# A planner's durations, a shared port and the readiness of q and k, in a transformer trunk whose attention heads are woven into its projections

## The chip, the cores and the metric

The kernel runs on one core of one Trainium2 chip. The metric is the device time of one execution in microseconds (us). Engines are called PE (TensorE), DVE (VectorE), ACT (ScalarE), POOL (GpSimd) and SP (SyncE, which only issues DMAs here).

## The reference

Two layers of a trunk on 512 tokens with 1024 features, in float32:

```python
for l in range(DEPTH):                                   # 2
    x = x + 0.5 * swiglu_ffn(x, ...)                     # 1024 -> 2816 -> 1024
    h = rms_norm(x, mix_norm[l])
    aq, ak, av, bq, bk, bv, cq, ck, cv, cg, gates = jnp.split(h @ w_in[l], split_points, axis=-1)
    y_a = diff_attention(qa, ka, va, lam, lam_init, a_subln[l])   # 4 heads, two softmaxes each, QK norm, rotary
    y_b = chunk_attention(qb, kb, vb, b_rel_bias[l])              # 8 heads, bias by distance, QK norm
    y_c = retention(qc, kc, vc, cg, c_out_norm[l])                # 4 heads, decay, output gate
    merged = (g[:, :, 0] * (y_a @ w_branch_a[l]) + g[:, :, 1] * (y_b @ w_branch_b[l])
              + g[:, :, 2] * (y_c @ w_branch_c[l]))               # g: sigmoid of the gate projections
    x = x + merged @ w_out[l]
    x = x + 0.5 * swiglu_ffn(x, ...)
```

y_a and y_c are normalised over the 128 features of each head before they are multiplied by their branch's weights.

## The kernel before

**Tiles.** Activations lie transposed, 128 features by 512 tokens to a tile. Each float32 operand is split into a high and a low part in fp32r, and each product becomes three matmuls: high by high, high by low, low by high (`mm3`, L230; in the profile bank<-xh,wh, xl,wh and xh,wl). The weights stream through SBUF once, in 422 chunks of 128x1024: SP loads a chunk (wr), ACT writes its high part (wh), DVE its low part (wl). Three chunks can be loaded ahead and three split (RAW, SPL). All 128x512 tiles come out of one ring of 72 (`big`, L170): a new tile is written only when everything that reads the tile 72 before it has ended, copies by DMA too. PE's results go to eight PSUM banks.

**Stages.** A layer is an FFN, a mixer and an FFN. The mixer (`mixer`, L914) makes the projections of q, k and v for A, then for B (`tokens`), then for the three branches. `branch` (L1029) first makes eight gate projections of 24 matmuls each; for branch 0 four projections of C's gates follow (`c_gates`: cg, cs); then come the branch's own matmuls over the four finished outputs ys, as bank<-yh,wh, yl,wh and yh,wl, three by four for each of eight output tiles. Between branch 0 and branch 1 the q, k and v of C are projected. At the end stands the projection by w_out.

**Side programs.** All that belongs to the heads is written as generators, which yield wherever they would wait:

- `prep` (L606) normalises and rotates the projected q or k (z), transposes it on PE (bank<-ident,z), splits it (qh, ql) and copies the halves by DMA into stacked tiles qk (`stack`, `twice`, copies at L661); `c_prep` (L997) does the same for C, with its copies at L1012.
- `a_head`, `b_head` and `c_head` (L775, L814, L849) multiply q by k, make the softmax or the decay (e, m, s), transpose it (bank<-ident,e to pt), multiply it by the values (vh, vl, or vv for B) and, for A and C, sum the squares of the output with a matmul against ones (`settle_head`).
- `finish` (L751) waits for a pair of heads, takes the inverse root of their sums of squares (ss; v, n, r, nine steps of 128x512 on DVE, `rsqrt_wide`), spreads it by DMA (rh<-r, L763), multiplies the heads' outputs by it (yu) and, for C, by the gate, and splits them (yh, yl). When the last pair is done it sets the flag yA or yC. B's heads set yB by themselves.

**What sets the order.** Every engine runs its instructions in the order in which they are written, and `Model` (L52) decides that order while the kernel is being built. It keeps a clock for each engine, adds a duration for each instruction (`note`, L89), and knows when each tile is ready (`ready`) and when a bank is free. After each projection matmul, `tick` (L249) lets a side program take a step if the model holds its operands for ready, if DVE and ACT are less than BACKLOG = 5000 ns behind PE, and if PE's pacing allows it. A step says what it waits for by what it yields: `then(...)`, `product(...)` with 1600 ns more, or `room(...)`, which asks for a free bank too and adds 800 ns. All of these are waits of the model; what an engine really waits for are the semaphores of its operands. A tile sent by DMA counts as ready 2500 ns after the latest of the clocks (`sent`, L85).

If the flag of a branch has not been set when its matmuls are due, `branch` calls `drain` (L301), which lets the side programs run with no projection matmul between them until the flag is there:

```python
if flag not in self.flags:
    self.drain(flag)
```

Of the kernel before, what the change touches and what calls it, by code (L numbers as in the profile page):

```python
# [35 lines left out]
class Queue:  # L36


    def __init__(self, model, name, engine):
        self.model, self.name, self.engine = model, name, engine  # L40
# [11 lines left out]
class Model:  # L52
# [3 lines left out]
    def __init__(self):  # L56
        self.t = dict(pe=0.0, dve=0.0, act=0.0, pool=0.0)
        self.wrote = {}
        self.read = {}
        self.slots = [0.0] * 8  # L60
        self.owner = {}

    @staticmethod
# [18 lines left out]
        end, by = max(self.read.get(self.key(ap), [(0.0, "pe")]))  # L82
        self.slots[self.owner.pop(self.key(ap))] = end + self.LAG[by]

    def sent(self, ap, wait=2500):  # L85

        self.wrote[self.key(ap)] = max(self.t.values()) + wait, "pe"

    def note(self, eng, op, named):  # L89
        aps = {k: a for k, a in named.items() if isinstance(a, bass.AP)}  # L90
        outs = [aps[k] for k in ("out", "accum_out") if k in aps]
        ins = [a for k, a in aps.items() if k not in ("out", "accum_out")]
        n = max(math.prod(a.shape[1:]) for a in outs[:1] + ins) if eng != "pe" else math.prod(outs[0].shape[1:])
        by_row = any(k in aps for k in ("scalar", "scalar1", "scale", "bias"))
        if "dma" in op:
            for a in outs:
                self.wrote[self.key(a)] = max(self.t[eng], self.t["pe"]) + 2500, eng
            return
        if eng == "pe":
            if op == "transpose":  # L100
                d = 109
            elif named["rhs"].dtype == F32R:
                d = n / 2.37 if n >= 256 else 213
            else:
                d = max(n, 64) * 1.7
        elif eng == "dve":
            plain = not any(a.space == bass.MemoryType.PSUM for a in ins + outs)
            d = 68 + n / (1.92 if op == "tensor_scalar" and plain else 0.96)
            d += 60 * by_row
        elif eng == "act":  # L110
            d = (50 if aps["in_"].space == bass.MemoryType.PSUM else 93) + n * 0.834 + 93 * by_row
        else:
            d = 100 + n * 2.2
        at = max([self.t[eng]] + [self.ready(a, eng) for a in ins])
        self.t[eng] = at + d
        for a in outs:
            self.wrote[self.key(a)] = at + d, eng
        for a in ins:
            if a.space == bass.MemoryType.PSUM:
                self.read.setdefault(self.key(a), []).append((at + d, eng))  # L120


def then(*aps):

    return aps, False, 0
# [7 lines left out]
def room(*aps):  # L133

    return aps, True, Kernel.MARGIN


class Kernel:
# [636 lines left out]
    def a_head(self, h, st):  # L775
        nc = self.nc
        es = self.weights()
        sums = {}

        def combine(i, e):  # L780
            s0, s1 = sums[i]
            for s in sums[i]:
                nc.vector.reciprocal(s, s)
            nc.vector.tensor_tensor(out=s1, in0=s1, in1=st["nlam"], op=ALU.mult)
            nc.vector.tensor_scalar(out=es[i], in0=es[i], scalar1=s0, scalar2=None, op0=ALU.mult)
            nc.vector.scalar_tensor_tensor(out=es[i], in0=e, scalar=s1, in1=es[i], op0=ALU.mult, op1=ALU.add)

        yield room(*(st[s][2 * h + c][0] for s in "qk" for c in range(2)))
        for i in range(NB + 1):
            if i < NB:  # L790
                bank = self.scores(st["q"][2 * h], st["k"][2 * h], i)
                yield then(bank)
                n = P * (i + 1)
                s = sums[i] = [self.small(1, "s") for _ in range(2)]
                self.softmax(bank, i, self.mask, s[0], es[i])
                yield room()
                bank = self.scores(st["q"][2 * h + 1], st["k"][2 * h + 1], i)
            if i:
                yield then(e)
                combine(i - 1, e)  # L800
            if i < NB:
                yield then(bank)
                e = self.big(F32, "e1")[:, 0:n]
                self.softmax(bank, i, self.mask, s[1], e)
                if i < NB - 1:
                    yield room()
        yield room(*es)
        pt = yield from self.transposed(es)
        yield "av"
        o = yield from self.values(pt, st["v"], slice(h * P, (h + 1) * P))  # L810
        yield from self.settle_head(o, st, h)
        self.flags.add(f"A{h}")

    def b_head(self, h, st):  # L814
        nc = self.nc
        tb = self.table()
        es = self.weights()
        yield room(*(st[s][h][0] for s in "qk"))
        for i in range(NB):
            bank = self.scores(st["q"][h], st["k"][h], i)  # L820
            yield then(bank)
            s = self.small(1, "s")
            e = es[i]
            self.softmax(bank, i, tb, s, e)
            yield then(e)
            nc.vector.reciprocal(s, s)
            nc.vector.tensor_scalar(out=e, in0=e, scalar1=s, scalar2=None, op0=ALU.mult)
            if i < NB - 1:
                yield room()
        self.fetch_table()  # L830
        yield room(*es)
        pt = yield from self.transposed(es)
        yield "bv"
        o = yield from self.values_b(pt, st["v"], h)
        if st["yu"][h // 2] is None:
            st["yu"][h // 2] = self.big(F32, "yb"), self.big(F32, "yb")
        y, t = st["yu"][h // 2]
        own, other = (slice(64 * i, 64 * i + 64) for i in (h % 2, 1 - h % 2))
        nc.scalar.activation(out=t[own], in_=o[other], func=AF.Copy)
        yield then(t)  # L840
        nc.vector.tensor_tensor(out=y[own], in0=o[own], in1=t[own], op=ALU.add)
        self.free(o)
        st["n"][h // 2] += 1
        if st["n"][h // 2] == 2:
            st["y"][h // 2] = yield from self.split_side(y)
            if None not in st["y"]:
                self.flags.add("yB")

    def c_head(self, h, st):  # L849
        nc = self.nc  # L850
        q, k = st["q"][h], st["k"][h]
        dt = self.table()
        pt = self.turned()
        yield room(q[0], k[0], k[1])
        for j in range(NB):
            bank = self.bank()
            n = S - j * P
            w = max(n, 256)
            o = slice(j * P, (j + 1) * P)
            self.dots(bank[:, 0:w], (k[0][:, o], k[1][:, o]), (q[0][:, S - w:S], q[1][:, S - w:S]))  # L860
            yield then(bank)
            if j < NB - 1:
                d = self.big(F32, "d")
                nc.vector.tensor_tensor(out=d[:, 0:n], in0=bank[:, 0:n], in1=dt[:, 0:n], op=ALU.mult)
                self.free(bank)
                hi, lo = pt[j]
                yield then(d)
                nc.scalar.activation(out=hi, in_=d[:, 0:n], func=AF.Copy)
                yield then(hi)
                nc.vector.tensor_tensor(out=lo, in0=d[:, 0:n], in1=hi.bitcast(F32), op=ALU.subtract)  # L870
            else:
                nc.vector.tensor_tensor(out=pt[j], in0=bank[:, w - n:w], in1=dt[:, 0:n], op=ALU.mult)
                self.free(bank)
            yield room()
        self.fetch_table()
        yield "cv"
        o = yield from self.values(pt, st["v"], slice(h * P, (h + 1) * P))
        yield from self.settle_head(o, st, h)
        self.flags.add(f"C{h}")
# [333 lines left out]
```

## Time and profile before

| | us |
|---|---|
| median of 3 runs | 2547.5 (2544.88 to 2548.47) |
| the profiled execution | 2552.16 |
| its span, from the first to the last instruction | 2550.4 |
| PE busy | 2517.2 |
| DVE busy | 1375.7 |
| ACT busy | 919.8 |
| POOL busy | 138.3 |

The mean clock granted to TensorE over the span is 0.996 of full speed. In rows of the timeline the columns are start, duration, engine, line, operation, out<-in, and in brackets the idle time ahead and what ended it. Most instructions have L48, the line of the helper through which all engines are called; they are told apart by their tiles. Rows of groups give the count, busy time and mean in ns of one, then the idle time before them.

### The profile page before, as it was taken

Reading aid. Unit: us, or ns where it says so; the run is one execution under the profiler, and the core shown is the slowest. Engines: PE = TensorE matmul, PEld = TensorE weight load, DVE = VectorE, ACT = ScalarE, POOL = GpSimd, SP = SyncE. Lnnn points to the kernel's source line nnn. Section 1 sums busy time; section 2 is a strip of 40 time slices with the busy share of each in tenths; the row PEclk is TensorE's granted clock in tenths of the full one; section 3 lists DMA queues with packets and bytes.
Section 4 is the critical chain, followed back from the end, with each engine's and each line's share of the span. In section 5 each row is a group of like instructions: output and inputs, shape, how many; then the busy total and the mean of one; then the engine's idle time right before and its main releaser. Section 6 shows DMA issues by size and latency. Waiting matters only on the chain.

```text
span 2550.4 us, 28931 instructions
## 1 busy us (share of the span) xinstructions
PE 2517.2 (99%) x11226; PEld 2054.4 (81%) x11226; DVE 1375.7 (54%) x2180; ACT 919.8 (36%) x1397; POOL 138.3 (5%) x104
## 2 busy tenths in 40 slices
PE   9999999999999999999999999999999999999999
PEld 7888887887878888888888888878878788888887
DVE  6334338776758653433353433477767576543332
ACT  4333224553443433332233332245534433333321
POOL 0000101000102100000000001010001021000000
PEclk9999999999999999999999999999999999999999
DMA  5333344527433433333333333344274324333332
GB/s 167 92 99 91 118 130 123 134 83 190 115 105 83 140 99 99 92 99 94 96 92 98 91 97 114 120 133 123 85 196 113 106 76 146 99 94 99 91 111 71
DMA packets 96617, 280.91 MB, mean 110 GB/s; under 512 B 13536, under 2 KB 14944, under 8 KB 96480
## 3 DMA queue, kind: packets, MB, share of 16 engines
q1 hardware_dynamic: 95760, 278.45, 38.2%
q8 instruction: 88, 1.44, 0.2%
q10 hardware_dynamic: 720, 0.62, 0.1%
q14 instruction: 49, 0.40, 0.0%
HBM read 237.08 MB, written 6.29 MB: 95 GB/s over the span
## 4 chain that ended last, share of the span: by engine, by line
PE 93%; DVE 3%; SPq 2%; DMA 1%; issue 0%; ACT 0%; DVEq 0%
PE bank L48 93%; SPq L661 1%; SPq L1012 1%; DVE wl L48 1%; DMA qk<-ql 1%; DVE e L48 0%; DMA x<-in_xt 0%; DVE n L48 0%; DVE g L48 0%; DVE z L48 0%; DVE pt L48 0%; DVE r L48 0%; DMA qk<-yh 0%; DVE ql L48 0%; ACT wh L48 0%
## 5 line engine op out<-in xcount | busy, mean ns | idle before, releaser
L48 DVE TENSOR_TENSOR wl<-wr,wh 128x1024 fp32r<-128x1024 f32 x422 | 530.8, 1259 | 705.7 <-ACT wh L48 703.6
L48 PE MATMUL bank<-xh,wh 128*128 128x512 f32 x1920 | 758.8, 395 | 0.0
L48 PE MATMUL bank<-xl,wh 128*128 128x512 f32 x1920 | 757.6, 395 | 0.1
L48 PE MATMUL bank<-xh,wl 128*128 128x512 f32 x1920 | 756.3, 394 | 0.0
L48 ACT ACTIVATE wh<-wr 128x1024 fp32r<-128x1024 f32 x422 | 445.4, 1056 | 775.2 <-PE bank L48 671.2
L48 PEld LDWEIGHTS bank<-xh,wh 128*128 128x128 f32 x1920 | 361.9, 188 | 78.2 <-ACT xh L48 1.2
L48 PEld LDWEIGHTS bank<-xl,wh 128*128 128x128 f32 x1920 | 362.0, 189 | 77.9 <-DVE xl L48 1.7
L48 PEld LDWEIGHTS bank<-xh,wl 128*128 128x128 f32 x1920 | 361.9, 188 | 77.7
L48 PE MATMUL bank<-ph,wh 128*128 128x512 f32 x704 | 276.6, 393 | 0.0
L48 PE MATMUL bank<-pl,wh 128*128 128x512 f32 x704 | 276.6, 393 | 0.0
L48 PE MATMUL bank<-ph,wl 128*128 128x512 f32 x704 | 276.6, 393 | 0.0
L48 PE MATMUL bank<-wl,xh 128*128 128x512 f32 x448 | 179.2, 400 | 0.0
L48 PE MATMUL bank<-wh,xh 128*128 128x512 f32 x448 | 178.8, 399 | 0.0
L48 PE MATMUL bank<-wh,xl 128*128 128x512 f32 x448 | 178.2, 398 | 0.0
L48 PEld LDWEIGHTS bank<-ph,wh 128*128 128x128 f32 x704 | 132.4, 188 | 29.6
L48 PEld LDWEIGHTS bank<-ph,wl 128*128 128x128 f32 x704 | 132.4, 188 | 29.4
L48 PEld LDWEIGHTS bank<-pl,wh 128*128 128x128 f32 x704 | 132.4, 188 | 29.4
L48 ACT ACTIVATE e<-e,m 128x128 f32<-128x128 f32 (+3 forms) x128 | 71.4, 558 | 118.8 <-DVE m L48 105.0
L48 ACT ACTIVATE t<-t 128x512 f32<-128x512 f32 x88 | 55.6, 632 | 162.5 <-DVE t L48 162.5
L48 POOL TENSOR_TENSOR acc<-acc,sq 128x512 f32<-128x512 f32 x30 | 39.4, 1314 | 1112.1 <-PE bank L48 567.7
L48 PEld LDWEIGHTS bank<-wh,xh 128*128 128x128 f32 x448 | 84.3, 188 | 17.0
L48 PEld LDWEIGHTS bank<-wl,xh 128*128 128x128 f32 x448 | 84.4, 188 | 16.8
(145 smaller groups left out, 2486.1 us busy)
## 6 DMA issues: line engine op xcount, KB each, us to landing
wr<-in_w SPq DMA_DIRECT2D x422, 512.0 KB, 3.6
qk<-qh SPq DMA_DIRECT2D x96, 128.0 KB, 4.2
qk<-ql SPq DMA_DIRECT2D x96, 128.0 KB, 3.8
xd<-x SPq DMA_DIRECT2D x16, 256.0 KB, 2.7
tb<-in_tbias SPq DMA_DIRECT2D x16, 256.0 KB, 3.3
rh<-r SPq DMA_DIRECT2D x32, 128.0 KB, 4.9
x<-xd SPq DMA_DIRECT2D x16, 256.0 KB, 5.6
qk<-yh SPq DMA_DIRECT2D x48, 64.0 KB, 2.0
```

What stands on the lines that cost most here:

```text
L48: return call(*args, **kw)
L661: self.nc.sync.dma_start(out=t[o].bitcast(F32), in_=x.bitcast(F32))
L1012: self.nc.sync.dma_start(out=t[at + 32 * i:at + 32 * i + 32].bitcast(F32), in_=x.bitcast(F32))
```

## The change

It touches the model and the first wait of each head; no instruction is added or removed, and every engine keeps its number of rows.

- The durations of `note` change for all engines. An example is DVE: an operation of 128x512 counted 68 + 512/0.96 = 601 ns and counts 130 + 512 * 1.1 = 693 ns; with a scalar per row 60 more in both.
- POOL's instructions, and DVE's with more than one operand in SBUF, go through one `port` in the model: one of them starts there only when the one before it has ended.
- A tile sent by DMA counts as ready after 4500 ns in place of 2500.
- A head's first scores wait, in the model, for every tile of its q and k, not for the first of each pair.

```diff
@@ class Model
+        self.port = []
...
-    def sent(self, ap, wait=2500):
+    def sent(self, ap, wait=4500):
...
+        in_sbuf = sum(x.space != bass.MemoryType.PSUM for x in ins)
...
-                d = n / 2.37 if n >= 256 else 213
+                d = max(n, 256) * 0.452
...
-            plain = not any(a.space == bass.MemoryType.PSUM for a in ins + outs)
-            d = 68 + n / (1.92 if op == "tensor_scalar" and plain else 0.96)
+            plain = in_sbuf == len(ins) and not any(a.space == bass.MemoryType.PSUM for a in outs)
+            d = 220 + n * 0.53 if op == "tensor_scalar" and plain else 130 + n * 1.1
             d += 60 * by_row
+            d += 85 * ("accum_out" in aps)
...
+        if eng == "dve" and in_sbuf > 1 or eng == "pool":
+            at = max([at] + [end for start, end in self.port if start <= at])
+            self.port = self.port[-7:] + [(at, at + d)]
         self.t[eng] = at + d
@@ a_head
-        yield room(*(st[s][2 * h + c][0] for s in "qk" for c in range(2)))
+        yield room(*(t for s in "qk" for c in range(2) for t in st[s][2 * h + c]))
@@ b_head
-        yield room(*(st[s][h][0] for s in "qk"))
+        yield room(*(t for s in "qk" for t in st[s][h]))
@@ c_head
-        yield room(q[0], k[0], k[1])
+        yield room(*q, *k)
```

The order changes in the mixer, in both layers in the same way. Three places of the first layer follow. Numbers behind the names tell buffers apart; they are counted through each kernel by itself.

**PE, ahead of branch 0.** bank<-xh,wh (with xl or wl) is a projection, ident,z a transpose of B's q or k, yh,wh the first matmul of the branch. Before:

```order
L48 MATMUL bank_4796<-ident,z_3802 128x128
L48 MATMUL bank_4796<-ident,z_3813 128x128
L48 MATMUL bank_4796<-ident,z_3824 128x128
L48 MATMUL bank_4796<-ident,z_3835 128x128
L48 MATMUL bank_4741<-xl_2525,wh_4650 128x512
L48 MATMUL bank_4741<-xh_2524,wl_4651 128x512
L48 MATMUL bank_4827<-yh_3935,wh_4690 128x512
L48 MATMUL bank_4827<-yl_3936,wh_4690 128x512
```

After:

```order
L48 MATMUL bank_4631<-xl_2525,wh_4504 128x512
L48 MATMUL bank_4631<-xh_2524,wl_4505 128x512
L48 MATMUL bank_4698<-ident,z_3433 128x128
L48 MATMUL bank_4698<-ident,z_3460 128x128
L48 MATMUL bank_4698<-ident,z_3471 128x128
L48 MATMUL bank_4698<-ident,z_3482 128x128
L48 MATMUL bank_4713<-ident,z_3433 128x128
L48 MATMUL bank_4713<-ident,z_3460 128x128
```

Twenty transposes follow one another from the third row shown to the branch's first matmul, with no projection among them. The last matmul of A's heads with ones stands 19 projection matmuls ahead of branch 0; before it stood 152 ahead. For branch 2 and C's heads it is 46 in place of 119.

**SP, the copies rh of the second pair of A's heads.** qk<-qh and qk<-ql are copies of B's q, wr<-in_w a weight chunk. Before:

```order
L661 DMA qk_4540<-qh_4512 64x512
L661 DMA qk_4540<-ql_4513 64x512
L763 DMA rh_4553<-r_4452 64x512 x2
L763 DMA rh_4556<-r_4452 64x512 x2
L195 DMA wr_4575<-in_w 128x1024
L661 DMA qk_4593<-qh_4544 64x512
```

After:

```order
L669 DMA qk_4718<-qh_4709 64x512
L669 DMA qk_4718<-ql_4710 64x512
L669 DMA qk_4721<-qh_4709 64x512
L669 DMA qk_4721<-ql_4710 64x512
L771 DMA rh_4728<-r_4671 64x512 x2
L771 DMA rh_4731<-r_4671 64x512 x2
L669 DMA qk_4734<-qh_4724 64x512
L669 DMA qk_4734<-ql_4725 64x512
```

After, the copies stand behind q pieces whose ql is written after r (the source of rh) on DVE. Behind them come four more copies of q and twelve of k before the next weight chunk.

**DVE, the end of the C heads.** r is the inverse root, g a gate projection's result, yu the output, yl its low part, wl a weight chunk's low part. Before:

```order
L48 TENSOR_SCALAR r_6791<-r_6791 128x512
L48 TENSOR_TENSOR g_6817<-bank_6770,rb_2602 128x512
L48 TENSOR_TENSOR g_6848<-bank_6823,rb_2602 128x512
L48 TENSOR_TENSOR wl_6821<-wr_6684,wh_6820 128x1024
L48 TENSOR_TENSOR wl_6852<-wr_6746,wh_6851 128x1024
L48 TENSOR_TENSOR g_6891<-bank_6857,rb_2602 128x512
L48 SCALAR_TENSOR_TENSOR yu_6617<-yu_6617,cols_74,rh_6863 128x512
L48 TENSOR_TENSOR yu_6617<-yu_6617,cs_4734 128x512
L48 TENSOR_TENSOR wl_6895<-wr_6787,wh_6894 128x1024
L48 TENSOR_TENSOR yl_6910<-yu_6617,yh_6909 128x512
```

After:

```order
L48 TENSOR_SCALAR r_6894<-r_6894 128x512
L48 TENSOR_TENSOR g_6919<-bank_6872,rb_2603 128x512
L48 TENSOR_TENSOR g_6950<-bank_6925,rb_2603 128x512
L48 SCALAR_TENSOR_TENSOR yu_6615<-yu_6615,cols_74,rh_6953 128x512
L48 TENSOR_TENSOR yu_6615<-yu_6615,cs_4624 128x512
L48 TENSOR_TENSOR yl_6962<-yu_6615,yh_6961 128x512
L48 SCALAR_TENSOR_TENSOR yu_6822<-yu_6822,cols_74,rh_6956 128x512
L48 TENSOR_TENSOR yu_6822<-yu_6822,cs_4690 128x512
L48 TENSOR_TENSOR yl_6968<-yu_6822,yh_6967 128x512
L48 TENSOR_TENSOR wl_6923<-wr_6792,wh_6922 128x1024
```

The weight splits wl and a gate result that stood between r and the heads' yl no longer do.

More of the change, by code (lines that the diff above doesn't have):

```diff
@@ L102, in note @@
             elif named["rhs"].dtype == F32R:
-                d = n / 2.37 if n >= 256 else 213
+                d = max(n, 256) * 0.452
             else:
-                d = max(n, 64) * 1.7
+                d = max(n, 64) * 1.72
         elif eng == "dve":
-            plain = not any(a.space == bass.MemoryType.PSUM for a in ins + outs)
-            d = 68 + n / (1.92 if op == "tensor_scalar" and plain else 0.96)
+            plain = in_sbuf == len(ins) and not any(a.space == bass.MemoryType.PSUM for a in outs)
+            d = 220 + n * 0.53 if op == "tensor_scalar" and plain else 130 + n * 1.1
             d += 60 * by_row
+            d += 85 * ("accum_out" in aps)
         elif eng == "act":
-            d = (50 if aps["in_"].space == bass.MemoryType.PSUM else 93) + n * 0.834 + 93 * by_row
+            d = (165 if aps["in_"].space == bass.MemoryType.PSUM else 207) + n * 0.834 + 93 * by_row
+            d += 187 * ("accum_out" in aps)
         else:
-            d = 100 + n * 2.2
+            d = 170 + n * 2.4
         at = max([self.t[eng]] + [self.ready(a, eng) for a in ins])
+        if eng == "dve" and in_sbuf > 1 or eng == "pool":
+            at = max([at] + [end for start, end in self.port if start <= at])
+            self.port = self.port[-7:] + [(at, at + d)]
         self.t[eng] = at + d
```

## The prediction, made before the result was known

> **What bounds the kernel now.** I read the page first, then PE's waits, the chain of waits, the groups by form, and the timeline at the places where the order changes.
>
> ```profile
> PE 2517.2 (99%) x11226; PEld 2054.4 (81%) x11226; DVE 1375.7 (54%) x2180; ACT 919.8 (36%) x1397; POOL 138.3 (5%) x104
> PE bank L48 <- DVE e L48: 17.4, 6, 5.2
> PE bank L48 <- DMA qk<-ql: 3.5, 6, 0.8
> PE bank L48 <- DVE z L48: 3.4, 2, 1.7
> PE bank L48 <- DMA qk<-qh: 1.4, 4, 0.6
> PE bank L48 <- DVE yl L48: 0.6, 2, 0.3
> 801.94 881.42 PE bank L48 x3821
> ```
>
> PE is busy for 99% of the span, and its waits (us in total, times, longest) are small: the first four rows are 25.7 us in both layers together. VectorE has 46% of the span free. So the time is PE's row of matmuls, and a new order can win back hardly more than those; it can lose as much as it makes PE wait. The last row, a piece of the chain (start, length), gives PE's pace: 881.42 / 3821 = 0.231 us for one matmul, mostly of 512 columns. By this I turn counts of matmuls in PE's order into time: what a wait has as cover.
>
> **The change part by part.** It adds no instruction and takes none away; it moves side programs (the heads' work) among the projection matmuls, in both mixers alike. I count one layer and double it. Its weight lies at the three branches: a branch's matmuls need four finished, normalised head outputs (yh, yl). Before, side work is spread so that projections stand behind the last head's work; after, all that is left of it stands in one block ahead of the branch, with nothing beside it on PE.
>
> The dependency that ends such a block is seen in the trace of before at branch 2, from the matmul with ones (the sum of squares) to the matmul with the last yl:
>
> ```profile
> 816.22 0.39 PE L48 MATMUL bank<-yh,ones 128*128 128x512 f32 x1
> 819.67 0.42 DVE L48 TENSOR_SCALAR v<-ss 128x512 f32<-128x512 f32 x1
> 820.66 0.69 DVE L48 SCALAR_TENSOR_TENSOR n<-r,v 128x512 f32<-128x512 f32 x1
> 827.20 0.43 DVE L48 TENSOR_SCALAR r<-r 128x512 f32<-128x512 f32 x1
> 831.55 2.43 SPq L763 DMA_DIRECT2D rh<-r  x4
> 837.54 0.75 DVE L48 SCALAR_TENSOR_TENSOR yu<-yu,cols,rh 128x512 f32<-128x512 f32 x1 [3.71 <-DMA rh<-r]
> 839.06 0.63 ACT L48 ACTIVATE yh<-yu 128x512 fp32r<-128x512 f32 x1 [3.61 <-DVE yu L48]
> 845.54 0.68 DVE L48 TENSOR_TENSOR yl<-yu,yh 128x512 fp32r<-128x512 f32 x1
> 846.28 0.51 PE L48 MATMUL bank<-yl,wh 128*128 128x512 f32 x1
> DMA to landing us min/median/max: 2.3/4.9/5.4
> L48 DVE SCALAR_TENSOR_TENSOR ql<-bank,cols,qh 128x512 fp32r<-128x512 f32 x16 | 11.9, 743 | 0.0
> L48 DVE SCALAR_TENSOR_TENSOR n<-y,v 128x32 f32<-128x32 f32 x24 | 4.6, 192 | 0.8
> L48 DVE TENSOR_TENSOR z<-z,y 128x512 f32<-128x512 f32 x32 | 23.3, 747 | 0.7
> 606.08 0.69 DVE L48 TENSOR_TENSOR cg<-bank,rb 128x512 f32<-128x512 f32 x1 [1.27 <-PE bank L48]
> 607.47 0.69 DVE L48 SCALAR_TENSOR_TENSOR cs<-cs,cg 128x512 f32<-128x512 f32 x1 [0.70 <-ACT cs L48]
> 415.06 0.49 PE L48 MATMUL bank<-ident,z 128*128 128x128 f32 x3
> ```
>
> The chain takes 846.28 - 816.22 = 30.1 us. Its parts: 3.45 to v; 0.99 to the nine steps of the inverse root; 827.20 - 820.66 = 6.54 for these, 0.73 each; the copies rh, whose landing takes 4.9 us in the median and 2.3 at least; then yu, yh and yl for two heads. Before hides it: 119 projection matmuls (27.5 us) and the first matmuls of the branch stand behind ones.
>
> *Branch 0 (yA).* After, only 19 projections (4.4 us) stand behind the last ones of the A heads; before it was 152 (35 us). From ones: v at 2.45 (the trace's 3.45 holds a weight split of about 1 us ahead of it on ACT), 0.99 and 6.54 to r, and among these the pair cg, cs with its 0.70 of waiting, 2.0 by its rows: 12.0. Then VectorE has three ql at 0.743 (14.2), eleven small steps of B's k norm at 0.19 (16.3) and four z at 0.747 (19.3). SP meanwhile stands with the two rh behind eight copies of q pieces that wait for these ql: I put the issue of rh at 17.1 to 18.3 and the landing, with 4.9, at 22.0 to 23.2. Then yu, yh, yl, the second yu, two ql, the second yl: 26.3; the matmuls of the first output tile end at about 26.8. Without a wait they would end at 4.4 + 3.0 (twenty transposes, three in 0.49 by the last row) + 2.8 (twelve matmuls) = 10.2. PE waits **16.6 us**; with the 2.3 us landing 14, and 20 if SP's copies take longer to get out of the way. The next weight chunk stands on SP behind twelve copies of B's k, but two chunks (48 matmuls, 11 us) are loaded by then, so I cost that at nothing; without this cover its landing of 4 us or so would be added.
>
> *Branch 2 (yC).* Behind the last ones of the C heads stand 46 projections (10.6 us), not 119. r is ready at 11.4 as in the trace (827.63 - 816.22). SP has nothing to wait for ahead of rh (in the trace it came to them only at 831.55): landing at 12.1 + 4.9 = 17.0. yu, product with the gate, yh and yl for two heads, now without weight splits between them: 22.7, first tile done at 23.2. Without waits 10.6 + 2.8 + 0.5 = 13.9. PE waits **9 us** (6.7 with a landing of 2.3, 10 as the other end).
>
> ```profile
> L48 DVE TENSOR_TENSOR pt<-bank,pt 128x512 fp32r<-128x512 f32 x24 | 16.4, 683 | 3.9 <-ACT pt L48 2.8 <-PE bank L48 1.1
> L48 ACT ACTIVATE yb<-bank 64x512 f32<-64x512 f32 x16 | 9.5, 593 | 22.7 <-PE bank L48 22.6
> L48 DVE TENSOR_TENSOR yb<-bank,yb 64x512 f32<-64x512 f32 x16 | 11.0, 686 | 5.6 <-ACT yb L48 5.5
> L48 DVE TENSOR_TENSOR yl<-yb,yh 128x512 fp32r<-128x512 f32 x8 | 5.5, 688 | 2.2 <-ACT yh L48 2.2
> ```
>
> *Branch 1 (yB).* The last B head's transposes, its seven products with vv and a C head's products stand in one block; before 41 projections (9.5 us) stood behind the products. The path runs through the copies pt (ACT, then VectorE 0.683), the products, yb 0.593 and 0.686, a split of about 0.6 and 0.688: some 4 us without the products. The C head's matmuls and the first nine of the branch (4 us) hide the part behind the products, but not the copies of pt. I take **3.5 us** (2 to 6).
>
> *The heads' start, which the planner now holds until all of q and k are there* (a wait in its model, none on an engine). Two convoys on SP make PE wait now:
>
> ```profile
> 603.97 1.11 SPq L661 DMA_DIRECT2D qk<-qh  x2
> 624.25 1.19 SPq L661 DMA_DIRECT2D qk<-ql  x2
> 623.58 0.42 DVE L48 CUSTOM_DVE_ANT_0 e<-bank,tb 128x256 f32<-128x256 f32 x1 [6.03 <-DMA qk<-ql]
> 631.89 0.46 PE L48 MATMUL bank<-ident,e 128*128 128x128 f32 x1 [2.61 <-DVE e L48]
> 690.78 2.42 SPq L1012 DMA_DIRECT2D qk<-yh  x4
> 708.74 2.42 SPq L1012 DMA_DIRECT2D qk<-yl  x4
> 709.23 0.75 DVE L48 SCALAR_TENSOR_TENSOR vl<-bank,rt,vh 128x512 fp32r<-128x512 f32 x1 [7.31 <-DMA qk<-yh]
> 710.63 0.47 PE L48 MATMUL bank<-ident,e 128*128 128x128 f32 x1 [5.10 <-DVE e L48]
> 417.27 0.33 PE L48 MATMUL bank<-ident,z 128*128 128x128 f32 x1 [1.72 <-DVE z L48]
> 631.90:635.40 3.50, 3.50 (x11) 0.51 0.35 89
> 710.60:714.10 3.50, 3.47 (x11) 0.53 0.68 173
> ```
>
> The 32 copies of B's k leave SP at 0.6 us each, 20 us in all; VectorE writes an e into a tile that a copy still reads, waits 6.03 us, and PE then waits for it. The new rule for `room` does not touch this wait, which is for the ring of tiles. Counted in matmuls at 0.231, the tile written has in the new order 2.8 us as cover from its last copy and not 6.5, but the e is needed 14.3 and not 9.9 us later; the two nearly balance: **+1** (0 to 4). In the convoy of C's pieces (690.78 to 711) the waiting writes have 6 to 7.5 us of cover in place of 10 to 12: **+2.5**, between -4, if its 5.10 us vanish for the most part, and +8. The first transposes of z come 18 matmuls (4.1 us) later, so that their wait of 1.72 goes: **-1.7**.
>
> *The clock.* After a PE wait of 3 to 5 us the granted clock is 0.51 and 0.53 for 3.5 us (the windows' rows: span, PE busy, clock), which costs 1.7 us. Most of the new slow matmuls fall into stretches where PE waits anyway, so I add **0.5**. The Trainium skill has this in "TensorE: Matmul & The Clock Gate", section "Why this matters": after an idle window of about 3.4 us the array runs at half rate until it has been busy for about as long; the trace agrees, with 0.51 and 0.53. Taken strictly, it speaks against this change: each idle of branches 0 and 2 would add its own 1.7 us, up to 6 us in all over the sum below.
>
> *Sum.* 16.6 + 3.5 + 9 + 1 + 2.5 - 1.7 + 0.5 = 31.4 us in a layer, 62.8 in two. The profiled execution took 2552.2 us (span 2550.4) and would take 2615; the median of the runs shown lies 4.7 us below it, so 2547.5 + 62.8 = **2610 us**. The FFN stages keep their order and cost nothing.
>
> The Trainium skill, "DMA: Bandwidth & Descriptors", section "Anatomy of one DMA", gives about 2.0 us fixed and 436 bytes per ns. For 64 KB that is an estimate of 2.15 us, beside the trace's 2.3 at least and 4.9 in the median. By the page the sum would be some 2600 us.
>
> **The rivals.**
>
> *SP's convoys grow (15%).* With weights queued behind the copies of k and of C's pieces, the block at branch 0 empties PE's banks for longer. For it: VectorE waits of 6.03 and 7.31 us in the trace and the shorter covers. Against it: e is needed later. One more wait of 5.10 at each of the two convoys adds 10 us a layer: 2630.
>
> *The blocks are cheaper (14%).* SP's queue is nearly empty in them, the copies land in 2.3 us and VectorE has nothing else: 12 + 2 + 6.5 a layer, less 1.7, the convoys as before: 18.8, 38 in all, 2585. Against it is the median of 4.9.
>
> *Faster (3%).* The waits for e, qk and z (25.7 us) vanish, since scores start with all of their operands present, and the blocks cost nothing: 2547.5 - 25.7 = 2522. It decides if the chain from ones to yl fits under its cover of 4.4 and 10.6 us; the row for it says 30.1, of which 6.54 are VectorE steps that depend on each other, so this cannot be made as small.
>
> *No change (2%).* The blocks cost what the vanished waits give: 20 to 30 us on both sides, 2547. It needs yA at a third of my sum.
>
> **How the numbers follow.** The forecast has 66%; with the bounds of its terms taken together (yA -2.6 and +3.4, yB -1.5 and +2.5, the convoys -6 and +8, yC -2.3 and +1, which will not all fall on one side) it lies at 2590 to 2626. To hold 8 in 10 the range reaches to the two rivals on either side: 2577 to 2636. A measurement can tell about 0.2% (5 us) from no change. Slower has 66 + 15 + 14 = 95%, no change 2%, faster 3%.
>
> **What would show it.** In the profile after, PE should wait for DVE yl (0.6 us before) some 50 us in all, in four pieces: two of 14 to 18 us ahead of branch 0, two of 6 to 10 ahead of branch 2; yA's wait should end with yl, behind a VectorE wait for rh; waits for pt or yl(yb) of 2 to 6 us should stand ahead of branch 1. The wait for z should be gone. The granted clock should fall to about 0.5 behind each block. It is wrong if PE's row shows no gap over 3 us ahead of the branches, or if the convoys' waits (DVE e) move by more than the blocks cost.

## The result, and the profile after

| | before | after |
|---|---|---|
| median, us | 2548.0 (2544.9 to 2549.2) | 2620.9 (2618.0 to 2623.4) |
| profiled execution, us | 2552.2 | 2619.4 |
| its span, us | 2550.4 | 2617.1 |
| mean clock granted to PE | 0.996 | 0.984 |

The ratio is 1.0288 (95% interval 1.0270 to 1.0305): 72.9 us slower. The forecast was 2610, with a range of 2577 to 2636. All times compare runs in the usual, fast state; one run of the kernel with VectorE's old durations, at 5076.8 us, is left out by that. The profile's page first, its line of busy time and the shares of the chain that ended last:

```profile
PE 2541.5 (97%) x11226; PEld 2068.5 (79%) x11226; DVE 1378.7 (53%) x2180; ACT 922.7 (35%) x1397; POOL 133.6 (5%) x104
PE 91%; DVE 4%; DMA 2%; SPq 2%; ACT 1%; issue 1%; POOL 0%; DVEq 0%; ACTq 0%
```

All engines do the same work; PE's share of the span falls by two points. PE's waits after (us in total, times, longest):

```profile
PE bank L48 <- DVE z L48: 27.6, 4, 10.9
PE bank L48 <- DVE m L48: 10.8, 4, 3.0
PE bank L48 <- ACT yh L48: 9.2, 4, 3.8
PE bank L48 <- DVE vl L48: 6.7, 2, 4.8
PE bank L48 <- DMA qk<-ql: 4.5, 6, 0.9
PE bank L48 <- DVE e L48: 2.9, 2, 1.5
PE bank L48 <- DVE pt L48: 2.6, 4, 1.1
PE bank L48 <- ACT pt L48: 2.2, 4, 0.8
```

These rows add up to 66.5 us; all of before's add up to 28.3. To see the clock as well, I add over all matmuls the time from one's start to the next one's start, less what the same form takes where nothing waits (0.231 us for 512 columns). This *lost PE time* is 39.9 us before and 106.9 after: 67.0 more, which is the 67.2 us between the profiled executions. By stretches of a layer:

| stretch | forecast | layer 1 | layer 2 |
|---|---|---|---|
| start of A's heads (z, first scores) | -1.7 | 4.35 to 8.46: +4.1 | 3.96 to 9.56: +5.6 |
| up to branch 0's first tile, with the clock | +17.1 | 0.0 to 14.60: +14.6 | 0.0 to 14.57: +14.6 |
| B's copies, first scores included | +1 | 9.92 to 12.95: +3.0 | 10.57 to 13.34: +2.8 |
| C's copies | +2.5 | 7.55 to 4.44: -3.1 | 8.05 to 7.55: -0.5 |
| branch 1 | +3.5 | 0.17 to 5.17: +5.0 | 0.17 to 5.16: +5.0 |
| branch 2 | +9 | 0.35 to 7.49: +7.1 | 0.16 to 7.77: +7.6 |
| sum | +31.4 | +30.7 | +35.0 |

Before, PE lost nothing up to branch 0's first tile, whose last matmul is the first row here; its next waits are those of B's scores for their copies:

```profile
608.86 0.39 PE L48 MATMUL bank<-yh,wl 128*128 128x512 f32 x1
609.81 0.35 PE L48 MATMUL bank<-qk,qk 128*128 128x256 f32 x1 [0.56 <-DMA qk<-qh]
610.91 0.35 PE L48 MATMUL bank<-qk,qk 128*128 128x256 f32 x1 [0.75 <-DMA qk<-ql]
```

**Branch 0.** The timeline from the last ones of A's heads to the last yl, and two windows (span, then busy time of PE, PEld, DVE, ACT and POOL, then the clock, the DMA engines' share and GB/s):

```profile
603.06 0.40 PE L48 MATMUL bank<-yh,ones 128*128 128x512 f32 x1
614.67 2.06 DVE L48 SCALAR_TENSOR_TENSOR ql<-bank,cols,qh 128x512 fp32r<-128x512 f32 x3
619.10 2.50 DVE L48 TENSOR_TENSOR z<-z,y 128x512 f32<-128x512 f32 x4
619.85 3.99 PE L48 MATMUL bank<-ident,z 128*128 128x128 f32 x12 [10.85 <-DVE z L48]
619.84 2.46 SPq L771 DMA_DIRECT2D rh<-r  x4
622.87 0.75 DVE L48 SCALAR_TENSOR_TENSOR yu<-yu,sub,rh 128x512 f32<-128x512 f32 x1 [1.27 <-DMA rh<-r]
626.90 0.68 DVE L48 TENSOR_TENSOR yl<-yu,yh 128x512 fp32r<-128x512 f32 x1
609.00:619.85 10.85, 0.00 (x1) 0.01 (x1) 9.64 (x24) 1.78 (x3) 0.00 (x0) 0.65 0.54 120
619.85:623.40 3.55, 3.17 (x11) 2.29 (x12) 2.28 (x4) 0.00 (x0) 0.00 (x0) 0.50 0.92 206
```

PE stands still for 10.85 us while VectorE works for 9.64 of them: the rest of the inverse root, the pair cg and cs, three ql, the small steps, z. The wait is put down to z and not to yl, because the transposes of z stand ahead of the branch in PE's row; they then run at a clock of 0.50, but yl is not there before 627.6 either.

**Branch 2.** The same chain behind C's ones, which were at 856.15:

```profile
866.82 0.43 DVE L48 TENSOR_SCALAR r<-r 128x512 f32<-128x512 f32 x1
867.31 2.39 SPq L771 DMA_DIRECT2D rh<-r  x4
870.26 0.75 DVE L48 SCALAR_TENSOR_TENSOR yu<-yu,cols,rh 128x512 f32<-128x512 f32 x1 [1.81 <-DMA rh<-r]
872.45 0.79 PE L48 MATMUL bank<-yh,wh 128*128 128x512 f32 x1 [3.77 <-ACT yh L48]
875.23 0.80 PE L48 MATMUL bank<-yh,wh 128*128 128x512 f32 x1 [0.83 <-ACT yh L48]
```

PE waits for yh twice, and the first tile ends 20.8 us after ones.

**B's copies.** VectorE and PE behind branch 0:

```profile
641.21 0.29 DVE L48 CUSTOM_DVE_ANT_0 e<-bank,tb 128x128 f32<-128x128 f32 x1 [8.97 <-DMA qk<-qh]
641.56 0.62 PE L48 MATMUL bank<-qk,qk 128*128 128x384 f32 x2 [2.57 <-DVE m L48]
649.11 0.42 DVE L48 CUSTOM_DVE_ANT_0 e<-bank,tb 128x256 f32<-128x256 f32 x1 [5.46 <-DMA qk<-qh]
649.60 1.06 PE L48 MATMUL bank<-qk,qk 128*128 128x512 f32 x2 [2.68 <-DVE m L48]
```

VectorE writes e into a tile that a copy still reads; it stands for 8.97 and 5.46 us with all that is queued behind it. PE's next scores, which read qk alone, then wait for m, the last thing read out of a score's bank: PE has run out of banks.

**The start.** The last steps of z in A's prep, on VectorE, POOL and PE, after:

```profile
413.69 6.13 POOL L48 TENSOR_TENSOR u<-z,tab 128x512 f32<-128x512 f32 x4 [16.45 <-ACT z L48]
417.16 2.94 DVE L48 TENSOR_TENSOR w<-z,tab 128x256 f32<-128x256 f32 x2
422.67 0.33 PE L48 MATMUL bank<-ident,z 128*128 128x128 f32 x1 [2.92 <-DVE z L48]
```

Two w take 2.94 us while POOL works; two others took 0.75, before and after. So z is ready later than its place in the order suggests, and PE's wait for it grows from 1.72 to 2.92.

### The profile page after: what moved, and what is told of

It is laid out like the page before. It is cut to its first block, busy times and chain, and to the rows that moved or that the text cites. A ratio compares the mean times of both kernels' runs of the same rounds, so it can differ in the third digit from the quotient of the medians.

```text
span 2617.1 us, 28956 instructions
## 1 busy us (share of the span) xinstructions
PE 2541.5 (97%) x11226; PEld 2068.5 (79%) x11226; DVE 1378.7 (53%) x2180; ACT 922.7 (35%) x1397; POOL 133.6 (5%) x104
## 4 chain that ended last, share of the span: by engine, by line
PE 91%; DVE 4%; DMA 2%; SPq 2%; ACT 1%; issue 1%; POOL 0%; DVEq 0%; ACTq 0%
PE bank L48 91%; SPq L669 1%; SPq L1020 1%; DMA qk<-qh 1%; DVE e L48 1%; DMA qk<-ql 0%; DVE z L48 0%; DVE n L48 0%; DMA rh<-r 0%; DVE wl L48 0%; DVE ql L48 0%; DVE yu L48 0%; DVE w L48 0%; DVE r L48 0%; DVE g L48 0%
## 5 line engine op out<-in xcount | busy, mean ns | idle before, releaser
L48 ACT ACTIVATE e<-e,m 128x512 f32<-128x512 f32 (+3 forms) x128 | 71.6, 560 | 140.8 <-DVE m L48 127.6
L48 PE MATMUL bank<-qk,qk 128*128 128x256 f32 (+2 forms) x320 | 83.3, 340 | 22.8 <-DVE m L48 10.8
L48 PEld LDWEIGHTS bank<-wh,xl 128*128 128x128 f32 x448 | 84.9, 190 | 17.8
```

Of the source, the lines that this page charges most:

```text
L48: return call(*args, **kw)
```

## The experiments

Theory 1 was the prediction's: side work piles up ahead of the branches, and PE waits out its chain. The rival was that the later start of heads and SP's queue of copies cost the time. Each run was timed against the kernel before on the same chip.

**The new durations alone.** `sent` back to 2500, no `port`, the old `room` lines:

```diff
-            at = max([at] + [end for start, end in self.port if start <= at])
...
-    def sent(self, ap, wait=4500):
+    def sent(self, ap, wait=2500):
```

> The kernel before with the new durations alone (no port, 2500 ns for a sent tile, heads start on the first tiles). Theory 1, the blocks: the new durations alone make side work pile up ahead of the branches. In its order a block of 20 transposes stands ahead of branch 0 with 53 projections behind the last ones (19 in the changed kernel), 23 side matmuls ahead of branch 1, and 73 projections behind C's last ones (46). By 0.231 us each that is 7.9 and 6.2 us more cover in a layer: 2621 - 28 = 2593 us, between 2578 and 2608. Theory 2, late readiness: what costs time is that heads start later (all tiles of q and k, 4500 ns) and run into SP's convoys of copies. Then this kernel, which has neither, is as fast as before: 2548, within 8.

2615.7 us, ratio 1.0261 (1.0237 to 1.0284). The rival falls as the cause of the whole: without late starts the loss is nearly as large. It may keep a part: behind B's copies PE loses some 5 us a layer here and 13 in the changed kernel, and other stretches lose more. The size that theory 1 gave was wrong too: 34 projections more as cover won nothing at branch 0, where PE loses some 18 us. The rows say why:

```profile
621.51 0.75 DVE L48 SCALAR_TENSOR_TENSOR yu<-yu,sub,rh 128x512 f32<-128x512 f32 x1 [3.52 <-DMA rh<-r]
625.47 3.04 PE L48 MATMUL bank<-ident,z 128*128 128x128 f32 x8 [14.53 <-DVE z L48]
```

Here VectorE's row has yu, which waits for rh, ahead of the steps to z, so the transposes ahead of the branch wait for the copy too. At branch 2, 27 projections more won nothing either: r was ready at 860.7, but SP stood behind a weight chunk and sent rh at 864.61. Counting from ones alone is not enough; what ends the block is all that VectorE and SP have in their rows ahead of its last step.

**All but the durations.** The old lines of `note` for all four engines, the rest of the change kept.

> The changed kernel with the old durations (port, 4500 ns and the wait for all of q and k stay). Theory 1: 120 and 142 projections stand behind the last ones of A and C, only 12 transposes stand ahead of branch 0 and no block ahead of branch 1, so the 14 + 5 + 7 us a layer of the branches are gone: 2548, between 2538 and 2565. Theory 2: the convoys and the waits for copies stay as in the changed kernel: 2600 or more.

2565.2 us, ratio 1.0067 (1.0043 to 1.0091): at the very end of theory 1's range, far from the rival. What it still costs is in part at branch 0: PE waits 5.6 us for yl (0.6 before), and once, at a matmul of yl, 5.1 us that the profile puts down to a copy of qh.

**VectorE's durations alone taken back:**

```diff
-            d = 220 + n * 0.53 if op == "tensor_scalar" and plain else 130 + n * 1.1
+            d = 68 + n / (1.92 if op == "tensor_scalar" and plain else 0.96)
             d += 60 * by_row
-            d += 85 * ("accum_out" in aps)
```

> The changed kernel with VectorE's old durations; those of PE, ACT and POOL, the port, 4500 ns and the wait for all of q and k stay. Theory 1: VectorE's durations alone make the blocks. In its order no block stands ahead of any branch, and 169 and 133 projections stand behind A's and C's last ones, so the branches cost nothing: 2552, between 2540 and 2568 (without any new duration 2565 was measured, with a block of 12 transposes left). Theory 2: the other parts together cost as much: 2580 or more.

2546.8 us, ratio 0.9994 (0.9982 to 1.0006): no difference from before. Without VectorE's new durations, all else in the change costs nothing in sum. PE has no wait for z or yh left; the largest that remain are for pt and e, behind the copies:

```profile
PE bank L48 <- ACT pt L48: 12.8, 2, 6.7
PE bank L48 <- DVE e L48: 8.1, 3, 4.3
711.43 0.42 DVE L48 CUSTOM_DVE_ANT_0 e<-bank,tb 128x256 f32<-128x256 f32 x1 [9.26 <-DMA qk<-yh]
```

That VectorE's durations would do it without those of the other engines was not run. The effects don't add: with all old durations 2565, with VectorE's alone 2547.

**The chain shortened, in both orders.** One Newton step of three in `finish`; r is less exact by that. The model counts the steps left out, so the order stays:

```diff
-            v.scalar_tensor_tensor(out=t, in0=y, scalar=-0.5, in1=val, ...)
+            v = self.nc.vector if step < real else planned
+            v.scalar_tensor_tensor(out=t, in0=y, scalar=-0.5, in1=val, ...)
```

> The changed kernel, in its own order, but the inverse root of the heads' sums (finish) makes one of its three Newton steps; six of its nine DVE instructions of 0.727 us are left out, 4.4 us for each pair of heads, and the model still counts them, so nothing else moves. Theory 1: the chain from ones through r to yl sets the end of the block at branch 0 and at branch 2, so PE's waits there get 4.4 us shorter each: 2621 - 4 x 4.4 = 2603, between 2598 and 2609. Theory 2: the chain is not what PE waits for: 2621, within 5.

> The kernel before, in its own order, with one of three Newton steps in finish (4.4 us of VectorE left out for each pair of heads, counted by the model all the same). Theory 1: before, the chain from ones to yl is hidden behind 119 and 152 projections, so nothing is won: 2548, within 6; the same cut won 16 us in the changed order. Theory 2: VectorE's load as such is what costs, before and after alike: 2548 - 16 = 2532.

2604.9 us in the changed order, 16.0 less than 2620.9; 2545.5 in the order before (ratio 0.9989, 0.9979 to 1.0000). The two waits in the changed order:

```profile
617.09 3.99 PE L48 MATMUL bank<-ident,z 128*128 128x128 f32 x12 [6.62 <-DVE z L48]
867.76 0.51 PE L48 MATMUL bank<-yh,wh 128*128 128x512 f32 x1 [1.46 <-ACT yh L48]
```

At branch 0, 10.85 has become 6.62, by 4.2 of the 4.4 us left out. At branch 2 PE's lost time fell by 1 to 2 us only: with r ready earlier, VectorE stood 3.85 us at a gate result g that waits for PE and lies ahead of yu in its row. The same steps of VectorE, for the second pair of A's and of C's heads, lie on PE's path in one order and are hidden in the other. This is the most direct evidence for theory 1, though its 4.4 us for each place holds at branch 0 alone, and the 16.0 near 4 x 4.4 is partly luck.

**Three heads at a time:**

```diff
-    HEADS = 2
+    HEADS = 3
```

> The changed kernel with three heads at a time in place of two (HEADS = 3). Theory 1: what lets side work pile up is that each head takes longer in the model and only two are under way. With three, no block stands ahead of branch 1, 142 projections stand behind C's last ones, and 43 (not 19) behind A's: 5 + 7.5 + 5.5 us a layer come back, 2621 - 36 = 2585, between 2570 and 2600. Theory 2: three heads hold more tiles of the ring and meet the copies more often: 2610 or more.

2615.4 us: theory 1 missed. The waits for yh and pt are gone, as it said, but branch 0 still loses some 12.5 us a layer, and other waits took the place of those gone:

```profile
PE bank L48 <- DVE m L48: 32.8, 9, 8.4
749.06 0.29 DVE L48 CUSTOM_DVE_ANT_0 e<-bank,tb 128x128 f32<-128x128 f32 x1 [13.98 <-DMA qk<-yh]
749.41 0.80 PE L48 MATMUL bank<-xh,wh 128*128 128x512 f32 x1 [8.40 <-DVE m L48]
```

**The copies on two queues.** Every second copy of q and k goes out on POOL's queue; the order is the changed one, or the one before:

```diff
-        for o, x in ((own, a), (other, b)):
-            self.nc.sync.dma_start(out=t[o].bitcast(F32), in_=x.bitcast(F32))
+        for q, o, x in ((self.nc.sync, own, a), (self.tc.nc.gpsimd, other, b)):
+            q.dma_start(out=t[o].bitcast(F32), in_=x.bitcast(F32))
```

> The changed kernel in its own order, but every second copy of q and k (qk) is issued on POOL's DMA queue and not on SP's. Theory 1, SP's convoy of copies at 0.6 us each holds the ring of tiles, and by it VectorE and PE (12.8 us of lost PE time a layer at 626 to 660 us, 4 to 7 at 720 to 764): with two queues the convoy lasts half as long, 8 + 4 us a layer come back, and rh leaves SP some 2 us earlier: 2621 - 24 = 2597, between 2586 and 2610. Theory 2, the copies wait for VectorE's ql rather than for the queue, or POOL is slower to issue them: 2621 or more.

> The same on the kernel before, in its own order. Theory 1: of its waits for e (17.4 us) and of the slow clock behind them (some 8 us) most vanish: 2548 - 20 = 2528, between 2520 and 2540. Theory 2: 2548 or more.

2598.9 us after, in theory 1's range; 2545.2 before (ratio 0.9980, 0.9964 to 0.9997), where it missed. After, the win is not shared out as theory 1 said: behind C's copies the lost time goes from 4.4 and 7.6 us to nothing (4 expected), behind B's it falls by 2 to 4 (8 expected). The DMA rows of the first show why the second queue doesn't halve the convoy (KB, then us to landing); in the changed kernel's own such copies land in 3.6 to 4.1:

```profile
qk<-qh SPq DMA_DIRECT2D x64, 128.0 KB, 6.1
qk<-ql POOLq DMA_DIRECT2D x64, 128.0 KB, 5.9
645.40 0.42 DVE L48 CUSTOM_DVE_ANT_0 e<-bank,tb 128x256 f32<-128x256 f32 x1 [3.48 <-DMA qk<-qh]
```

Issued faster, each copy took longer to land. VectorE's wait of 5.46 us falls to 3.48 only, and that of 8.97 stays.

**Both, three heads and two queues:**

> The changed kernel with three heads at a time and every second copy of q and k on POOL's queue. With three heads alone 2615 us were measured, PE's waits for m being 32.8 us in nine. Theory 1: three heads do take away the blocks of branches 1 and 2, and what took their place is SP's convoy of copies; with two queues half of the waits for m goes, and the slow clock behind them: 2615 - 22 = 2593, between 2580 and 2604. Theory 2: three heads need more of VectorE at once, and the queues don't matter: 2612 or more.

2584.6 us: the waits that three heads brought were those for SP's copies. At C's copies VectorE now stands 6.36 us in place of 13.98:

```profile
PE bank L48 <- DVE m L48: 9.2, 8, 1.5
728.84 0.29 DVE L48 CUSTOM_DVE_ANT_0 e<-bank,tb 128x128 f32<-128x128 f32 x1 [6.36 <-DMA qk<-yh]
```

**u on VectorE.** In A's prep, still counted for POOL by the model:

```diff
-                nc.gpsimd.tensor_tensor(out=uu, in0=zz, in1=bc(cs, 0, 64), op=ALU.mult)
+                self.tc.nc.vector.tensor_tensor(out=uu, in0=zz, in1=bc(cs, 0, 64), op=ALU.mult)
```

> The changed kernel in its own order, but the rotary product u of A's prep runs on VectorE and not on POOL (the model still counts it for POOL). Theory 1: PE's wait for z at 422 us (2.92 us, and 3 to 4 more of slow clock and late scores) comes from POOL and VectorE getting in each other's way: w takes 1.47 us beside POOL and 0.38 alone, POOL's u 1.5 each. Without POOL the last z is ready some 3 us earlier and the wait goes: 2 x 4 us less, 2613, between 2608 and 2618. Theory 2: the wait comes from the place of the instructions alone, and VectorE's four more products (0.7 us each) make it longer: 2621 to 2630.

2612.2 us, 8.7 less. PE's four waits for z are down to the two ahead of branch 0, and two w take 0.75 again:

```profile
PE bank L48 <- DVE z L48: 21.7, 2, 10.9
416.05 0.75 DVE L48 TENSOR_TENSOR w<-z,tab 128x256 f32<-128x256 f32 x2
```

The lost time of the start falls from 8.46 to 3.89 us, and so shows the cause of that row of the table: from 413.75 two steps to z and two w took VectorE 6.4 us beside POOL's u, and the same four take 2.1 here, with 0.7 for the u that is added. The Trainium skill states the mechanism in "SBUF — State Buffer", section "SBUF: two separate sides": a VectorE operation with two inputs in SBUF and a GpSimd operation lock each other out for a whole instruction. The trace agrees, with 1.47 us for a w of 0.38.

**Towards a faster kernel.** The order before, u on VectorE, and only B's and C's copies on two queues:

> The kernel before, in its own order, with every second copy of B's and C's q and k on POOL's queue (A's stay on SP) and the rotary product u on VectorE. Theory 1: with all copies on two queues PE lost 37.0 us in the trace, hardly less than the 39.9 before, because POOL was late with u and A's first copies (7.2 us at 443 to 493, 2.3 before); without that some 10 us more come back: 2535, between 2527 and 2542. Theory 2: the waits move on to the next operand however the copies go out: 2543 to 2550.

2538.1 us, ratio 0.9949 (0.9928 to 0.9969), as theory 1 had it. Behind C's copies PE now loses under 0.3 us a layer (7.55 and 8.05 before); B's cost no less than they did. The same on the changed kernel with VectorE's old durations:

> The changed kernel with VectorE's old durations (as in the run that took 2547), every second copy of B's and C's q and k on POOL's queue, and u on VectorE. In that run PE lost 34.5 us over its matmuls' own time: 10 us a layer at 713 to 757 us behind C's copies and 9 at 610 to 639 behind B's. Theory 1: with two queues most of the first and half of the second go, as in the kernel before with two queues: 2547 - 20 = 2527, between 2519 and 2537, faster than both kernels. Theory 2: two queues win no more than the 9.5 us that they won on the kernel before: 2537 or more.

2538.8 us, ratio 0.9954 (0.9937 to 0.9971). Both beat the kernel before by half a per cent and the changed one by 3. Theory 1 missed on the second, and theory 2 had it: the two queues and u on VectorE together won 8 us there, about as much as on the order before. PE still waits 7.2 us for e, and copies on POOL's queue land late:

```profile
PE bank L48 <- DVE e L48: 7.2, 2, 4.0
qk<-qh POOLq DMA_DIRECT2D x16, 128.0 KB, 7.4
```

## Why the prediction was right, and where it was not

**The direction and the mechanism were right.** The blocks ahead of the three branches make +26.7 and +27.2 us of the two layers' +30.7 and +35.0, and the shortened chain shows that they wait on VectorE's steps. The faster case and "no change" needed a chain of 30 us to fit under covers of 4.4 and 10.6 us, and it did not.

**Branch 0** was forecast at 16.6 and half a us of clock, and cost 14.6 in both layers. The size that was off is the landing of rh: VectorE began yu 3.03 us after the issue (619.84 to 622.87), where I had taken the median of 4.9. With 3.03 the working puts the last yl 24.4 us behind ones and not 26.3; it came at 24.5. The end that the prediction named, yl behind rh, was that of the last matmuls. The long wait itself was for z, in the transposes that stand ahead of the branch. So one sign failed: "some 50 us" of waits for DVE yl were named, and the waits were 21.7 us for z and 9.2 for yh. "The wait for z should be gone" failed too.

**Branch 2** was forecast at 9 and cost 7.1 and 7.6. The same landing was mis-sized: yu began 2.95 us after the issue. With 2.95 the working gives 9 - 1.95 = 7.1. That it fits so well is partly luck, for rh also left 0.9 us sooner than forecast, and slow matmuls behind the last yl cost 1.1. The median of before held copies that stood in a busy queue; the bound of 2.3 was the nearer row. The prediction's estimate of 2.15 us is for 64 KB, but the rh copies are of 128 KB, for which the same formula of the Trainium skill ("DMA: Bandwidth & Descriptors", "Anatomy of one DMA") gives an estimate of 2.3 us; that section is on DMAs issued by GpSimd, and these are issued by SP.

**Branch 1** was forecast at 3.5 and cost 5.0, within its bounds.

**B's copies** were forecast at "+1 (0 to 4)" and cost 3.0 and 2.8, within the bounds but by another path. I had asked only when the transposes need e, and PE's waits for e did fall, from 17.4 to 2.9 us. But VectorE, standing on a tile that a copy still reads, also doesn't read the scores' banks, so PE waited 10.8 us for m (0.5 before), ahead of the transposes. C's copies went the other way (-3.1, -0.5), within the bounds. So the rival that let both convoys grow by 10 us a layer missed: together they cost -0.1 and +2.3.

**The start is the step that failed,** in sign: "their wait of 1.72 goes", and it cost 4.1 and 5.6 more. The order showed when PE asks for z, and I took z's own time as unchanged. In the new order its last steps run beside POOL's four u, and each w takes 1.47 us.

**The clock** fell to 0.50 behind the blocks of branches 0 and 2, as the Trainium skill's rule on idle windows ("TensorE: Matmul & The Clock Gate", "Why this matters") has it. At branch 0 this added nothing behind the last yl, for the slow matmuls ran while it was still missing. At branch 2 they ran on behind it, at 875.9, up to 878.3: 1.1 us in each layer, where the sum had 0.5 for all. Behind B's copies the waits of 2.57 and 2.68 us are shorter than the 3 us that the rule names, and the clock was 0.53 for some 3 us after each all the same: here the trace goes against the rule. These slow matmuls are some 3 us of the 12.95 there.

The sum of 62.8 us against the 67.2 of the profiled executions is partly luck: over both layers, 9 us too much at C's copies, 5 at branch 0 and 3 at branch 2 stand against 13 too little at the start, 4 at B's copies and 3 at branch 1. The medians lie 72.9 us apart, 6 more than the profiled executions; what differs in the other executions isn't in this trace and stays open. The profiled executions of other kernels differ even where nothing waits: from one undisturbed matmul of 512 columns to the next it was 0.2304 us on average in before and 0.2305 after, but 0.2297 with VectorE's old durations and 0.2318 with three heads. Over some 10,000 of them 1 ns is 10 us, so a difference of a few us between two kernels here need not come from their waits. What sets this pace, one trace of each doesn't tell.

**What of the change did it?** VectorE's new durations, by the run that took them alone back; which of their parts was not run. That they are the truer ones (601 ns counted before for what takes 692 in the trace, 693 now) did not help: my reading is that the planner keeps two heads under way, and with longer steps the same rules let less side work through before a branch. That three heads take the blocks of branches 1 and 2 away fits this, but which rule holds the side work back is not shown.

## What to carry to other kernels

A truer number in a planner's model is a new order, which can be a worse one, and the order has to be read before it is believed. Where such a change moves work, look at what stands in one block ahead of a consumer with no filler beside it, and add up all that the slowest engine has in that block, what it waits for in order included. Take a transfer's time from rows where its queue was as empty as it will be. A wait of one engine for a buffer spreads through everything queued behind it, so ask not only who needs its result but also which banks it no longer frees.

## What the runs showed of the hardware that was not expected

- A VectorE product of 128x256 with two operands in SBUF took 1.47 us beside a POOL instruction and 0.38 without; POOL's own u took 1.5 us each in that stretch.
- Copies of 64 rows of 2 KB on two queues at once landed in 5.9 to 7.1 us at the median of each group, in place of 3.6 to 4.1 on one queue. Two queues won 22 us where PE waited for them most, 2 us in the order before, and 8 to 9.5 with u on VectorE and A's copies left on SP.
- In layer 2 of the kernel before, four waits of PE of 0.17 to 0.77 us, between 1880.7 and 1884.3, were followed by seven matmuls 0.43 us apart at a granted clock of 0.50; in layer 1 the same four waits were followed by a clock of 1.00.
